# Six pairs ahead of the seven-product stage, its operands formed on VectorE, and other slots for adaLN and down

## The chip, the cores and the metric

The kernel runs on one core of a Trainium2 chip. The metric is the device time of one execution in microseconds (us), lower is better. The engines are TensorE (PE in the rows, PEld for its weight loads), VectorE (DVE), ScalarE (ACT), GpSimd (POOL) and SyncE (SP), whose queue issues nearly all DMAs here.

## The reference

Two layers of a diffusion trunk, width 1024, on 1024 latent tokens and, in layer 0, 256 context tokens. All matmuls around the change are in float32 accuracy.

```
mod = silu(c) @ w_ada[i] + b_ada[i]            # adaLN: shifts, scales, gates; 1024 x 6144
h = h + gt1 * mixer_i(modulate(rms_norm(h)))   # sliding-window attention, then neighbourhood attention
a = modulate(rms_norm(h), g_ffn, sh2, sc2)
gu = a @ w_gate_up[i]                          # 1024 x 5632
h = h + gt2 * ((silu(gu[:, :2816]) * gu[:, 2816:]) @ w_down[i])
```

## The kernel before

Activations are kept transposed: 128 channels on the partitions, 512 tokens in a row. An accurate float32 product is made of three fp32r matmuls: `split` (L140, L141) makes of a tile a high part (ScalarE's cast) and a low part (a subtraction on VectorE or GpSimd, by its argument `lo`), and low times low is left out.

**Gate and up** of the latent tokens are one product of 2 x 2 blocks (gate and up by the two halves of the channels; the two halves of the channels by the two halves of the tokens), done in seven products instead of eight. The operands on the token side are made once per layer: B11 and B21 are the normalized token half 0 (`norm_lat(0)`), T2, T3, T1, T4 and B22 are sums and differences of both halves (`norm_lat(1)`, L876 to L892, and `combine`, L894 on), each of four tiles. `f` runs over 22 pairs of a gate and an up tile. `first` makes two products (with B11 and B21), `second` one (T2), `third` four (T3, T1, T4, B22); `weights(f)` forms the weight side. A product (`product`, L793) is twelve 512-column matmuls. The first `NPRE` pairs run `first` ahead of the operand forming in program order, so that TensorE has work meanwhile; their results are held in `kp` tiles.

**Down** (L1041) takes the pairs in groups of two and then four; for each group and each half of the tokens it makes eight output tiles (steps), twelve matmuls each (six in the first group), and VectorE adds each to `h` out of its bank (`gate`, L833), of which there are four (`bm`).

**adaLN** of layer 1 (`ada`, L153) runs in layer 0's down by `tick`, one k-tile of 128 rows at a time: two DMAs of 512 KB, and four matmuls of 32 columns that fill the four column strips of the array (`j`), each recorded as two. adaLN of layer 0 runs the same way in the first stage.

SBUF tiles come from pools by tag, with a fixed number of slots: `wsp` 12 (weights), `pr` 16 (token operands), `px` 11 (`xslot`), `raw` and `rawf` 3 each (loads), `prc`/`kp` 8. T2, T3, B11 and B21 take `pr`, T1, T4 and B22 `wsp`. A compile-time planner orders the instructions of each engine: with its own model of durations it takes, at each moment, the instruction that comes first in the program among those whose inputs and slots are ready. The chip then runs each engine's and each queue's list in that order, with waits on semaphores.

Of the kernel before, what the change touches and what calls it, by code (L numbers as in the profile page):

```python
# [19 lines left out]
P = 128  # L20
# [32 lines left out]
class Trunk:  # L53
# [7 lines left out]
    def setup(self):  # L61
# [32 lines left out]
        self.hc = dr.tile([D, CTX], F32, name="hc_s")  # L94
        self.ss = [dr.tile([NF, P, SEQ], F32, name=f"s{i}_s") for i in range(2)]
# [24 lines left out]
    def unit(self, src, lo="vector", after=None, raws=None):  # L120
        nc = self.nc
        ws = []
        for i in range(2):
            s = slice(512 * i, 512 * i + 512)
            r = raws[i]() if raws else self.raw()
            if after is not None:
                nc.gpsimd.tensor_copy(out=r[0:1, 0:1], in_=after[0:1, 0:1])
            nc.sync.dma_start(out=r, in_=src[:, s])
            ws.append(self.split(r, self.slot(), lo))
        return ws  # L130
# [14 lines left out]
    def ada(self, layer, grp):  # L145
        ps = self.bank()
        for k in range(KT):
            ts = [self.slot(F32) for _ in range(2)]
            for y, t in enumerate(ts):
                self.nc.sync.dma_start(out=t.rearrange("p j n -> p (j n)"),  # L150
                                       in_=self.a["w_ada"][layer, k * P:(k + 1) * P, grp * 2048 + 1024 * y:grp * 2048 + 1024 * y + 1024])
            for j in range(4):
                self.nc.tensor.matmul(ps[32 * j:32 * j + 32, :], self.cond[:, k, :], ts[j // 2][:, j % 2], start=(k == 0), stop=(k == KT - 1))  # L153
            yield
        self.ada_close(layer, grp, ps, [(j, (32 * j, 32 * j + 2)) for j in range(4)])
        yield
# [639 lines left out]
    def back(self, layer, o):  # L796
# [68 lines left out]
        def norm_lat(c):  # L865
# [17 lines left out]
            for j in range(4):  # L883

                nc.scalar.activation(out=h[1, j], in_=h[1, j], func=AF.Identity, bias=sh[:, j, 0:1])
                nc.gpsimd.tensor_tensor(out=h[0, j], in0=h[1, j], in1=h[0, j], op=ALU.subtract)
                t2 = tmp()
                nc.vector.scalar_tensor_tensor(out=t2, in0=h[1, j + 4], scalar=sh[:, j + 4, 0:1], in1=h[0, j],
                                               op0=ALU.add, op1=ALU.subtract)
                B["t2", j] = t2  # L890
                B["T2", j] = self.split(t2, self.pslot(), alt(j))
                nc.scalar.activation(out=h[1, j + 4], in_=h[1, j + 4], func=AF.Identity, bias=sh[:, j + 4, 0:1])  # L892
                yield

        def combine():
            for j in range(4):
                nc.vector.tensor_tensor(out=h[1, j], in0=h[1, j + 4], in1=h[1, j], op=ALU.subtract)
                B["T3", j] = self.split(h[1, j], self.pslot(), alt(j))
                yield
            for j in range(4):  # L900
                B["T1", j] = self.split(h[0, j], self.slot(), alt(j))
                yield
            for j in range(4):
                nc.vector.tensor_tensor(out=h[0, j + 4], in0=h[0, j + 4], in1=B["t2", j], op=ALU.subtract)
                B["T4", j] = self.split(h[0, j + 4], self.slot(), alt(j))
                yield
            for j in range(4):
                B["B22", j] = self.split(h[1, j + 4], self.slot(), alt(j))
# [83 lines left out]
        NPRE = 3  # L992
# [11 lines left out]
        U = [first(f, ew[f]) for f in range(NPRE)]  # L1004
        w0 = weights(0)
        s0 = next(w0)
# [4 lines left out]
        for f in range(NF):  # L1011
            w = weights(f) if f else iter((s0, *w0))
            u = U[f] if f < NPRE else first(f, next(w))
# [4 lines left out]
        if not last:  # L1018
            self.later = [self.ada(1, i) for i in range(3)]
# [42 lines left out]
        for g in groups:  # L1062
            W = {f: self.unit(a["w_down"][layer, f * P:(f + 1) * P, :], "gpsimd") for f in g}
            for c in range(2):
                acts = {}
                for f in g:
                    r = rawf()
                    nc.sync.dma_start(out=r, in_=self.ss[layer][f, :, c * 512:(c + 1) * 512])
                    w = self.split(r, self.pslot(), "gpsimd")
# [3 lines left out]
                for nt in range(KT):  # L1073
# [6 lines left out]
                    if n % 3 == 0:  # L1080
# [174 lines left out]
```

## Time and profile before

| | |
|---|---|
| median of 3 runs | 2980.5 us (2977.04 to 2981.38) |
| the profiled execution | 2978.35 us, span 2976.6 us |
| TensorE busy | 2873.6 us, 97% |
| VectorE / ScalarE / GpSimd busy | 51% / 38% / 42% |
| mean granted TensorE clock | 0.986 |
| DMA | 392.66 MB, 132 GB/s in the mean |

The shares are means over stages with different limits. A busy TensorE is not yet one at its peak: after a wait its clock can be granted low, and the same matmuls take longer. A row of the order in time gives the start, the length, the engine, the line, the operation, the tile written and those read, the count, and in brackets the idle time before it and what ended that. "x" before a number counts instructions.

### The profile page before, as it was taken

The numbers are of one execution on the slowest core, as the hardware profiler recorded it, in microseconds if no ns is written. First come the engines' busy times: TensorE is split into PE (matmuls) and PEld (weight loads), VectorE is DVE, ScalarE is ACT, GpSimd is POOL, SyncE is SP. The second block draws the span as 40 slices with busy tenths as digits, with TensorE's granted clock in tenths as the row PEclk, the third lists the DMA queues.
The fourth block names the chain that finished last, engine by engine and source line by source line (L and its number), as shares of the span: only waits on it lengthen the run. The fifth ranks groups of instructions, "written<-read, shape, count | busy, mean of one in ns | idle before, by whom it ended". The sixth has DMA issues, their size and how long they took to land.

```text
span 2976.6 us, 42736 instructions
## 1 busy us (share of the span) xinstructions
PE 2873.6 (97%) x15586; PEld 2308.6 (78%) x15586; DVE 1525.0 (51%) x2643; ACT 1124.3 (38%) x2263; POOL 1237.0 (42%) x1124
## 2 busy tenths in 40 slices
PE   5999999997999999999999999999998899999999
PEld 3667767786888886778998888777787788887887
DVE  5656777558555442226543344266656755553222
ACT  4323666434332232224553223266644333323120
POOL 3443242127544545433873354011103755556440
PEclk8999999998999999999999999999999999999999
DMA  7573342531222247544553464366652222226321
GB/s 261 195 220 92 96 127 75 169 112 60 89 82 80 83 145 258 195 166 136 184 187 106 131 168 120 118 156 160 179 172 97 82 85 84 83 82 196 94 89 61
DMA packets 299843, 392.66 MB, mean 132 GB/s; under 512 B 29424, under 2 KB 165104, under 8 KB 299632
## 3 DMA queue, kind: packets, MB, share of 16 engines
q1 hardware_dynamic: 230736, 351.37, 37.2%
q10 hardware_dynamic: 68896, 38.55, 4.5%
q8 instruction: 123, 2.02, 0.3%
q14 instruction: 88, 0.72, 0.1%
HBM read 310.39 MB, written 79.43 MB: 131 GB/s over the span
## 4 chain that ended last, share of the span: by engine, by line
PE 84%; DVE 7%; DMA 4%; POOL 2%; issue 1%; ACT 1%; SPq 1%; DVEq 0%; ACTq 0%; POOLq 0%
PE bm L1041 16%; PE b L793 14%; PE bm L793 11%; PE bm L343 10%; PE bm L851 7%; PE bm L1102 4%; PE b L589 3%; PE b L343 3%; PE b L579 2%; PE b L731 2%; PE b L1041 2%; PE b L716 2%; DMA qst<-q_s 2%; PE b L153 2%; PE b L688 1%
## 5 line engine op out<-in xcount | busy, mean ns | idle before, releaser
L1041 PE MATMUL bm<-pr,wsp 128*128 128x512 f32 x2112 | 493.8, 393 | 4.5 <-DVE px L833 4.5
L1041 PEld LDWEIGHTS bm<-pr,wsp 128*128 128x128 f32 x2112 | 396.3, 189 | 111.6 <-DVE px L833 23.3
L793 PE MATMUL b<-wsp,px 128*128 128x512 f32 x1584 | 379.5, 393 | 2.8 <-DVE kp L1139 2.8
L793 PE MATMUL bm<-pr,px 128*128 128x512 f32 x1440 | 356.5, 396 | 19.3 <-DVE pr L141 11.1
L833 DVE SCALAR_TENSOR_TENSOR px<-bm,mod,px 128x512 f32<-128x512 f32 (+1 forms) x232 | 171.1, 741 | 388.6 <-PE bm L1041 336.0
L793 PEld LDWEIGHTS b<-wsp,px 128*128 128x128 f32 x1584 | 299.2, 189 | 69.5 <-DVE kp L1139 3.6
L141 POOL TENSOR_TENSOR wsp<-raw,wsp 128x512 fp32r<-128x512 f32 x186 | 241.4, 1308 | 249.2 <-ACT wsp L140 231.6
L141 POOL TENSOR_TENSOR px<-wt,px 128x512 fp32r<-128x512 f32 x176 | 237.9, 1364 | 243.1 <-ACT px L140 235.7
L793 PEld LDWEIGHTS bm<-pr,px 128*128 128x128 f32 x1440 | 272.7, 190 | 82.3 <-DVE pr L141 12.9
L140 ACT CAST wsp<-raw 128x512 fp32r<-128x512 f32 x302 | 184.9, 619 | 342.1 <-PE bm L1041 99.9
L343 PE MATMUL bm<-wsp,pr 128*128 128x512 f32 x1152 | 272.4, 393 | 0.0
L343 PEld LDWEIGHTS bm<-wsp,pr 128*128 128x128 f32 x1152 | 213.5, 188 | 43.3
L140 ACT CAST px<-wt 128x512 fp32r<-128x512 f32 x176 | 108.6, 621 | 349.0 <-PE b L793 319.0
L851 PE MATMUL bm<-pr,wsp 128*128 128x512 f32 x768 | 176.8, 390 | 0.0
L283 POOL TENSOR_TENSOR hrs<-hss,mhalf 128x8 f32<-128x8 f32 (+1 forms) x66 | 104.3, 1581 | 172.3 <-DVE hss L281 170.5
L141 POOL TENSOR_TENSOR pr<-rawf,pr 128x512 fp32r<-128x512 f32 x88 | 114.4, 1318 | 134.9 <-ACT pr L140 133.7
L343 PE MATMUL b<-wsp,pr 128*128 128x512 f32 x576 | 150.4, 414 | 18.3 <-ACT pr L252 6.1
L851 PEld LDWEIGHTS bm<-pr,wsp 128*128 128x128 f32 x768 | 143.3, 188 | 29.3
L343 PEld LDWEIGHTS b<-wsp,pr 128*128 128x128 f32 x576 | 110.3, 197 | 58.6 <-issue 13.3
L696 DVE CUSTOM_DVE_ANT_0 pr<-b,wsp,big 128x640 f32<-128x640 f32 (+1 forms) x128 | 107.5, 846 | 87.3 <-PE b L691 86.5
L141 POOL TENSOR_TENSOR px<-raw,px 128x512 fp32r<-128x512 f32 x76 | 110.2, 1452 | 91.6 <-ACT px L140 91.6
L1139 DVE TENSOR_TENSOR t<-b,kp 128x512 f32<-128x512 f32 x88 | 60.3, 685 | 169.3 <-PE b L793 169.3
(198 smaller groups left out, 4869.5 us busy)
## 6 DMA issues: line engine op xcount, KB each, us to landing
wsp<-w_ada SPq DMA_DIRECT2D x96, 512.0 KB, 6.2
qst<-q_s SPq DMA_DIRECT2D x288, 128.0 KB, 3.1
raw<-w_gu SPq DMA_DIRECT2D x144, 256.0 KB, 2.7
rawf<-w_gu SPq DMA_DIRECT2D x132, 256.0 KB, 3.0
raw<-w_down SPq DMA_DIRECT2D x110, 256.0 KB, 3.0
s_s<-t SPq DMA_DIRECT2D x88, 256.0 KB, 2.0
rawf<-s_s SPq DMA_DIRECT2D x88, 256.0 KB, 3.1
raw<-w_qkv SPq DMA_DIRECT2D x72, 256.0 KB, 3.3
```

The costliest lines, as they stand in the source:

```text
L140: self.nc.scalar.copy(out=w[:, 0, :n], in_=x)
L141: getattr(self.nc, lo).tensor_tensor(out=w[:, 1, :n], in0=x, in1=f32(w[:, 0, :n]), op=ALU.subtract)
L283: nc.gpsimd.tensor_tensor(out=rs[:, :nh], in0=ss[:, :nh], in1=self.mhalf[:, :nh], op=ALU.pow)
L343: self.nc.tensor.matmul(ps, x, y, start=(k == 0 and i == 0), stop=(k == KT - 1 and i == 2))
L589: nc.tensor.matmul(op[64 * r:64 * r + 64, :256], u["v"][:, kt, :], u["pt"][i][:, 256 * r:256 * r + 256], start=(i == 0), stop=(i == len(kt ...
L696: nc.vector.tensor_tensor_reduce(out=pt[:, :nl + 256], in0=V, in1=u["bias"][x][m // 7][:, b0:b0 + nl + 256], scale=-1.0, scalar=self.big, ...
L793: self.nc.tensor.matmul(ps, x, y, start=first and k == 0 and i == 0, stop=last and k == 3 and i == 2, skip_group_check=True)
L833: nc.vector.scalar_tensor_tensor(out=h[c, k], in0=ps, scalar=mod[:, ty, k, z:z + 1], in1=h[c, k], op0=ALU.mult, op1=ALU.add)
L851: nc.tensor.matmul(ps[:, :n], x, y, start=(k == 0 and i == 0), stop=(k == KT - 1 and i == 2))
L1041: nc.tensor.matmul(ps, x, y, start=(z == 0 and i == 0), stop=(z == len(parts) - 1 and i == 2))
L1102: nc.tensor.matmul(ps[:, q * CTX:(q + 1) * CTX], x, y, start=(k == 0 and i == 0), stop=(k == KT - 1 and i == 2))
L1139: self.nc.vector.tensor_tensor(out=out, in0=x, in1=y, op=op)
```

## The change

`norm_lat(1)` forms the difference of the two halves in one VectorE instruction from the shifted sum, instead of ScalarE and GpSimd, and all splits of T2, T3, T1, T4 and B22 put their subtraction on VectorE (`alt` put every second one on GpSimd). `NPRE` goes from 3 to 6: pairs 3 to 5 store their two tiles in device memory and load them back in the loop. Pair 0's weights are no longer begun ahead of the operand forming. `ada` can take several k-tiles at a time and another slot tag; its matmuls begin with the tile that is loaded last, and the others are held behind that one. Layer 1's adaLN takes two k-tiles at a time, from `pr`, at every fifth step of down instead of every third. In down, the weights of pairs 0 and 1 take `pr` slots instead of `wsp`, and the splits alternate between GpSimd and VectorE.

```diff
+        self.us = [dr.tile([NF, 2, P, 512], F32, name=f"u{i}_s") for i in range(2)]
...
-    def unit(self, src, lo="vector", after=None, raws=None):
+    def unit(self, src, lo="vector", after=None, raws=None, slot=None):
...
-            ws.append(self.split(r, self.slot(), lo))
+            ws.append(self.split(r, (slot or self.slot)(), lo))
...
-    def ada(self, layer, grp):
+    def ada(self, layer, grp, slot=None, n=1):
         ps = self.bank()
-        for k in range(KT):
-            ts = [self.slot(F32) for _ in range(2)]
-            for y, t in enumerate(ts):
-                self.nc.sync.dma_start(out=t.rearrange("p j n -> p (j n)"),
-                                       in_=self.a["w_ada"][layer, k * P:(k + 1) * P, grp * 2048 + 1024 * y:grp * 2048 + 1024 * y + 1024])
-            for j in range(4):
-                self.nc.tensor.matmul(ps[32 * j:32 * j + 32, :], self.cond[:, k, :], ts[j // 2][:, j % 2], start=(k == 0), stop=(k == KT - 1))
+        for k0 in range(0, KT, n):
+            ts = {}
+            for k in range(k0, k0 + n):
+                for y in range(2):
+                    ts[k, y] = (slot or self.slot)(F32)
+                    self.nc.sync.dma_start(out=ts[k, y].rearrange("p j n -> p (j n)"),
+                                           in_=self.a["w_ada"][layer, k * P:(k + 1) * P, grp * 2048 + 1024 * y:grp * 2048 + 1024 * y + 1024])
+            with ExitStack() as order:
+                for k in range(k0 + n - 1, k0 - 1, -1):
+                    for j in (2, 3, 0, 1):
+                        m = self.nc.tensor.matmul(ps[32 * j:32 * j + 32, :], self.cond[:, k, :], ts[k, j // 2][:, j % 2],
+                                                  start=(k == n - 1), stop=(k == KT - n))
+                        if k == k0 + n - 1 and j == 2:
+                            order.enter_context(self.tc.issue_after(getattr(m, "ins", m)))
...
-                nc.scalar.activation(out=h[1, j], in_=h[1, j], func=AF.Identity, bias=sh[:, j, 0:1])
-                nc.gpsimd.tensor_tensor(out=h[0, j], in0=h[1, j], in1=h[0, j], op=ALU.subtract)
+                nc.vector.scalar_tensor_tensor(out=h[0, j], in0=h[1, j], scalar=sh[:, j, 0:1], in1=h[0, j],
+                                               op0=ALU.add, op1=ALU.subtract)
...
-                B["T2", j] = self.split(t2, self.pslot(), alt(j))
-                nc.scalar.activation(out=h[1, j + 4], in_=h[1, j + 4], func=AF.Identity, bias=sh[:, j + 4, 0:1])
+                B["T2", j] = self.split(t2, self.pslot(), "vector")
+                for k in (j, j + 4):
+                    nc.scalar.activation(out=h[1, k], in_=h[1, k], func=AF.Identity, bias=sh[:, k, 0:1])
...
-                B["T3", j] = self.split(h[1, j], self.pslot(), alt(j))
+                B["T3", j] = self.split(h[1, j], self.pslot(), "vector")
...
-        NPRE = 3
+        NPRE, HELD = 6, 3
...
-        U = [first(f, ew[f]) for f in range(NPRE)]
-        w0 = weights(0)
-        s0 = next(w0)
+        U = []
+        for f in range(NPRE):
+            U.append(first(f, ew[f]))
+            if f >= HELD:
+                for i in range(2):
+                    nc.sync.dma_start(out=self.us[layer][f, i], in_=U[f][i])
...
-            w = weights(f) if f else iter((s0, *w0))
-            u = U[f] if f < NPRE else first(f, next(w))
+            w = weights(f)
+            if f >= NPRE:
+                u = first(f, next(w))
+            elif f < HELD:
+                u = U[f]
+            else:
+                u = keep(), keep()
+                for i in range(2):
+                    nc.sync.dma_start(out=u[i], in_=self.us[layer][f, i])
...
-            self.later = [self.ada(1, i) for i in range(3)]
+            self.later = [self.ada(1, i, self.pslot, 2) for i in range(3)]
...
-            W = {f: self.unit(a["w_down"][layer, f * P:(f + 1) * P, :], "gpsimd") for f in g}
+            W = {f: self.unit(a["w_down"][layer, f * P:(f + 1) * P, :], alt(f), slot=self.slot if f > 1 else self.pslot) for f in g}
...
-                    w = self.split(r, self.pslot(), "gpsimd")
+                    w = self.split(r, self.pslot(), alt(f + 1))
...
-                    if n % 3 == 0:
+                    if n % 5 == 0:
```

The splits of T1, T4 and B22 change as that of T3 does.

## Rows read from the trace of the kernel before

**Rows 1.** The page's first part: busy us, share of the span, instructions.

```profile
PE 2873.6 (97%) x15586; PEld 2308.6 (78%) x15586; DVE 1525.0 (51%) x2643; ACT 1124.3 (38%) x2263; POOL 1237.0 (42%) x1124
```

**Rows 2.** Busy time in equal stretches of 50 us: the stretch, its length, then busy us and instructions of PE, PEld, DVE, ACT and POOL, the granted TensorE clock, the DMA engines' busy share and GB/s. The start of down in layer 0, the head of the seven-product stage in layer 1, and an undisturbed stretch of the seven-product stage.

```profile
1100.00:1150.00 50.00, 45.95 (x196) 31.54 (x195) 17.22 (x23) 15.91 (x28) 28.15 (x22) 0.97 0.90 313
2300.00:2350.00 50.00, 37.04 (x134) 28.13 (x135) 47.92 (x43) 21.47 (x39) 43.35 (x27) 0.83 0.17 58
2400.00:2450.00 50.00, 50.00 (x220) 41.01 (x220) 26.48 (x30) 16.01 (x28) 26.43 (x20) 1.00 0.26 90
```

**Rows 3.** The same columns, for the head of the seven-product stage in layer 0 and in layer 1, and for the operand chain on VectorE in layer 1.

```profile
670.98:746.62 75.64, 60.14 (x239) 46.07 (x238) 63.76 (x64) 33.26 (x59) 56.51 (x36) 0.89 0.19 63
2278.85:2354.95 76.10, 60.68 (x242) 46.90 (x240) 63.36 (x62) 32.67 (x57) 55.65 (x35) 0.89 0.19 66
2291.27:2326.46 35.19, 21.30 (x64) 14.60 (x62) 35.19 (x30) 21.23 (x37) 29.37 (x19) 0.76 0.02 8
```

**Rows 4.** TensorE in order of time, the head in layer 1 (L784: the transposes that release the chain).

```profile
2278.85 6.96 PE L793 MATMUL bm<-pr,wsp 128*128 128x512 f32 x30
...
2286.46 4.33 PE L793 MATMUL bm<-pr,wsp 128*128 128x512 f32 x18
2290.63 0.60 PE L784 MATMUL b<-ident,rs 128*128 128x128 f32 x4
...
2295.16 3.04 PE L793 MATMUL bm<-pr,wsp 128*128 128x512 f32 x12 [1.16 <-ACT kp L951]
...
2302.10 1.65 PE L793 MATMUL bm<-pr,px 128*128 128x512 f32 x3 [3.33 <-POOL pr L141]
2308.97 2.93 PE L793 MATMUL bm<-pr,px 128*128 128x512 f32 x6 [5.22 <-DVE pr L141]
2311.69 0.63 PE L793 MATMUL b<-pr,px 128*128 128x512 f32 x1
```

**Rows 5.** TensorE in order of time, the head in layer 0 (L774 at 659.42: the sums of the latent norm).

```profile
659.42 0.95 PE L774 MATMUL b<-ones,acc 128*128 128x2 f32 x8
...
670.98 6.08 PE L793 MATMUL bm<-pr,wsp 128*128 128x512 f32 x26
...
677.26 5.24 PE L793 MATMUL bm<-pr,wsp 128*128 128x512 f32 x22
682.34 0.60 PE L784 MATMUL b<-ident,rs 128*128 128x128 f32 x4
```

**Rows 6.** VectorE in order of time, the operand chain in layer 1.

```profile
2291.27 5.36 DVE L876 SCALAR_TENSOR_TENSOR px<-px,gsc,b 128x512 f32<-128x512 f32 x8 [3.87 <-PE b L784]
...
2308.84 0.68 DVE L897 TENSOR_TENSOR px<-px 128x512 f32<-128x512 f32 x1
2309.44 1.77 DVE L904 TENSOR_TENSOR px<-px,t 128x512 f32<-128x512 f32 x1
```

**Rows 7.** GpSimd in order of time, the same stretch.

```profile
2295.71 1.30 POOL L141 TENSOR_TENSOR wsp<-px,wsp 128x512 fp32r<-128x512 f32 x1 [0.26 <-ACT wsp L140]
...
2300.34 1.71 POOL L141 TENSOR_TENSOR pr<-t,pr 128x512 fp32r<-128x512 f32 x1
```

**Rows 8.** TensorE in order of time, the start of down in layer 1.

```profile
2727.58 3.79 PE L1041 MATMUL bm<-pr,wsp 128*128 128x512 f32 x16
2735.82 29.39 PE L1041 MATMUL bm<-pr,wsp 128*128 128x512 f32 x116 [4.45 <-DVE px L833]
```

**Rows 9.** VectorE in order of time, the same place.

```profile
2733.60 1.50 DVE L1139 TENSOR_TENSOR t<-t,kp 128x512 f32<-128x512 f32 x1 [5.13 <-ACT t L988]
2735.03 2.71 DVE L833 SCALAR_TENSOR_TENSOR px<-bm,mod,px 128x512 f32<-128x512 f32 x4
```

**Rows 10.** ScalarE in order of time, the same place.

```profile
2732.42 0.62 ACT L140 CAST wsp<-raw 128x512 fp32r<-128x512 f32 x1 [1.28 <-DMA raw<-w_down]
2732.95 0.62 ACT L988 ACTIVATE t<-t 128x512 f32<-128x512 f32 x1
```

**Rows 11.** TensorE in order of time, down in layer 0: the start, two stretches of four column matmuls, then one of eight.

```profile
1127.09 1.78 PE L153 MATMUL b<-wsp,cond 128*32 128x512 f32 x4 [4.05 <-DMA wsp<-w_ada]
...
1137.74 1.05 PE L153 MATMUL b<-wsp,cond 128*32 128x512 f32 x4
1138.73 1.67 PE L1041 MATMUL bm<-pr,wsp 128*128 128x512 f32 x6
...
1256.68 8.46 PE L1041 MATMUL bm<-pr,wsp 128*128 128x512 f32 x36
1265.07 1.06 PE L153 MATMUL b<-wsp,cond 128*32 128x512 f32 x8
1266.06 8.46 PE L1041 MATMUL bm<-pr,wsp 128*128 128x512 f32 x36
```

**Rows 12.** TensorE in order of time, the first stage: two k-tiles of adaLN one behind the other.

```profile
168.42 1.92 PE L153 MATMUL b<-wsp,cond 128*32 128x512 f32 x16
170.28 3.48 PE L343 MATMUL b<-wsp,pr 128*128 128x512 f32 x14
```

**Rows 13.** L153 alone in two stretches, the first stage and layer 0's down: length, busy us and instructions of PE and PEld, granted clock, DMA share, GB/s.

```profile
100.00:222.00 122.00, 24.30 (x128) 3.75 (x128) 1.00 0.77 239
1119.00:1352.00 233.00, 31.49 (x192) 4.43 (x192) 0.99 0.59 200
```

**Rows 14.** Whom ScalarE waited for from 1100 to 1360 us (layer 0's down): us in total, times, the longest.

```profile
ACT pr L140 <- DMA rawf<-s_s: 46.7, 13, 9.5
```

More of the change, by code (lines that the diff above doesn't have):

```diff
@@ L897, in combine @@
                 nc.vector.tensor_tensor(out=h[1, j], in0=h[1, j + 4], in1=h[1, j], op=ALU.subtract)
-                B["T3", j] = self.split(h[1, j], self.pslot(), alt(j))
+                B["T3", j] = self.split(h[1, j], self.pslot(), "vector")
                 yield
             for j in range(4):
-                B["T1", j] = self.split(h[0, j], self.slot(), alt(j))
+                B["T1", j] = self.split(h[0, j], self.slot(), "vector")
                 yield
@@ L904, in combine @@
                 nc.vector.tensor_tensor(out=h[0, j + 4], in0=h[0, j + 4], in1=B["t2", j], op=ALU.subtract)
-                B["T4", j] = self.split(h[0, j + 4], self.slot(), alt(j))
+                B["T4", j] = self.split(h[0, j + 4], self.slot(), "vector")
                 yield
             for j in range(4):
-                B["B22", j] = self.split(h[1, j + 4], self.slot(), alt(j))
+                B["B22", j] = self.split(h[1, j + 4], self.slot(), "vector")
                 yield
```

## The prediction

> **What bounds the kernel now.** I read the page first: TensorE is busy for 97% of the span [rows 1], so a change can only win where TensorE waits, where its clock is granted low, or where it does work twice. The table of busy time in equal stretches then shows where that is. An undisturbed 50 us hold 220 matmuls at a granted clock of 1.00 [rows 2], which is 50 / 220 = 0.2273 us for each 512-column matmul, 2.73 us for a product of twelve. Two kinds of stretch fall short: the head of the seven-product stage in each layer (0.83 in one of them) and the start of the down stage, where the DMA engines are at 0.90 [rows 2].
>
> In the head, from the first matmul of pair 0's first product on, I asked for one stretch in each layer [rows 3]. Each holds three pairs' first two products and thirteen more products, 19 x 12 = 228 large matmuls, or 51.8 us, and about 1 us of small ones. They take 75.64 and 76.10 us, at a mean granted clock of 0.89. So **23 us are lost per layer**. [...]
>
> What TensorE waits for is a chain on VectorE that is busy without a pause from 2291.27 to 2326.46: 30 instructions in 35.19 us, beside 29.37 us of GpSimd [rows 3]. The two get in each other's way: a VectorE subtraction takes 0.68 us (0.60 from start to start) with GpSimd idle and 1.77 beside it [rows 6], a GpSimd one 1.30 or 1.71 [rows 7].
>
> **The chain without GpSimd.** The change gives VectorE all twenty subtractions of `split` (ten before) and folds the four GpSimd subtractions of L886 into four fused VectorE instructions. VectorE then has 16 fused ones (8 of L876, 4 new, 4 of L888) at 5.36 / 8 = 0.67 us and 28 plain ones at 0.60 [rows 6]: 10.7 + 16.8 = 27.5 us, against 35.2. GpSimd keeps only weight splits there, and most of those wait for an `xslot` that T4's operands free. From the chain's start the operands are ready at 13.1 us (T2: 16 x 0.67 + 4 x 0.60), 17.9 (T3), 20.3 (T1), 25.1 (T4) and 27.5 (B22).
>
> [...] Rows price the same subtraction at 1.30 on one engine and 0.60 on the other, so I count on the shorter chain.
>
> **More cover.** Pairs 3 to 5 move their first two products (six products, 16.4 us) ahead of the chain's results; TensorE's work stays the same in all. How much of the twelve products still lies behind the chain's start decides. The chain starts when four transposes (L784) have run, and these come after the products in program order. In both layers they ran after exactly 48 matmuls [rows 4, 5], in layer 0 although the sums that they need were taken 11 us before the first product. So the planner puts them where it finds no product ready. With three pairs that was where a second product waited for ScalarE to empty its bank (1.16 us in the trace [rows 4]). With six pairs pair 3's first product fills that hole; the next holes are after five products or, once four banks are in use, after seven. So the chain starts 13.6 + 1.2 = 14.8 us after the first product, or 20.3, against 12.4 now.
>
> Behind the start lie then seven products (19.1 us) or five (13.6), with some three waits of 1.16 us, 3.5 in all, at the end, where nothing is left to fill them. T2 (13.1) is hidden in both. In the late case TensorE ends the pairs at 17.1, T2's product at 19.8, T3's and T1's at 25.3; T4's adds into a bank that VectorE must first read, two additions that queue behind the chain, at 28.7: a wait of 3.4, and some 3 us at low clock after it. Loss 3.5 in the early case, 9.9 in the late one, against 23. I take 7: **16 us saved per layer, 32 in all**, bounds 26 and 39. Its other costs are hidden: six stores and six loads of 256 KB per layer and six weight halves loaded twice lie where the DMA engines are at 0.26 [rows 2]; the stores wait on SP for ScalarE's evacuation, with weight loads queued behind them, which are needed only after twelve products. The extra VectorE subtractions for pairs 3 to 5 fall before the chain. If GpSimd worked through the chain after all, the price is that of the second rival.
>
> **Down's start.** In layer 1 TensorE stops for 4.45 us with all four banks full, and the next 116 matmuls take 29.39 us instead of 26.4 [rows 8]: 7.5 us. The bank is late because VectorE's product of the stage before waited 5.13 us for ScalarE's Silu [rows 9], which stood behind a cast waiting for a `w_down` load [rows 10]. That load was late because its weights take `wsp` slots, which T1, T4 and B22 hold to the stage's end. Pairs 0 and 1 of `w_down` now take `pr` slots, which B11 and B21 leave with the last pair's second product. I take 6 us saved, bounds 0 (another cast blocks the Silu) and 7.5. In layer 0 the same hole is 4.05 us, ended by a `w_ada` load [rows 11], with some 2 us at low clock after it: 6. But adaLN tiles are now asked for 2.1 MB at a time, one batch in five steps of 1.36 us, 308 GB/s where the DMA engines move 313 at 0.90 [rows 2]; a wait for them can come back. I take 3, bounds -6 and 6. The splits that move from GpSimd to VectorE cost nothing while four banks cover VectorE; the last rival prices that.
>
> **adaLN.** A stretch of eight column matmuls takes 0.99 us from start to start, and a stretch of four, half a k-tile, takes 0.99 too [rows 11]. Torn tiles cost twice. In down the 31.49 us of L153 [rows 13] are 29 such stretches for 24 tiles. Each also costs the neighbours 0.21 us (36 matmuls take 8.39 us between two stretches, 8.18 undisturbed [rows 11]). Two tiles together took 1.85 us [rows 12]. So 29 x 1.20 = 34.8 becomes 12 x 2.06 = 24.7: 10 us. I take 8, since part of it lies in the hole counted above, bounds 4 and 10. In the first stage 24.30 us for 16 tiles [rows 13] could become 16 x 0.99 = 15.8, 8 us less; but TensorE also waits for VectorE and loads there, so I take 4, bounds 0 and 8.
>
> **The sum.** 32 + 6 + 3 + 8 + 4 = 53 us off the profiled execution's 2978.35 gives 2925.4. The median of the runs is 2.15 above that execution: **2927 us**. All bounds at their best give 70.5 off, 2910; all at their worst 24 off, 2956.
>
> **Rivals.** (1) The transposes come after all twelve products. Nothing is then behind the chain's start: TensorE waits 13.1 for T2, 2.1 for T3, 2.6 for T4, with 3.5 between pairs and some 8 at low clock, 29 instead of 23. The head loses 12 instead of winning 32: 2971. For it: they are last in program order; against it: in both layers they found a hole. 0.12. (2) The chain stays at 35 us, because weight splits on GpSimd keep running beside it: 7.5 more per layer, 2942. For it: GpSimd's 29.37 us now; against it: 14 of its 19 instructions there are the ones that move. 0.13. (3) The head wins, but adaLN and down do not, because layer 0's down start is set by the DMA engines (0.90) and the first stage by its loads: 2948. For it: both holes there end with a load; against it: torn stretches are TensorE's own time. 0.13. (4) Slower: in down VectorE now holds splits that wait for loads, and the emptying of the banks queues behind them. ScalarE waited 46.7 us for such loads in 13 waits there, up to 9.5 [rows 14]; three free banks cover 3 x 2.73 = 8.2 us. If each of the 24 half groups of both layers lost 2.2 us, the 53 would be gone; at 3 us the time is 2999. The mean wait of 3.6 speaks against it. 0.05.
>
> **Chances and range.** The forecast has 0.57. The range of 2908 to 2958 leaves out the first and last rivals and little else. This kernel's runs tell a difference of about 0.2%, 6 us, from none. Faster by more: the forecast, rivals 2 and 3 and most of rival 1, 0.91; within it 0.04; slower 0.05.
>
> **What the profile after would show.** Right: L784 after 60 to 84 matmuls of products; VectorE's subtractions in the head at 0.68 us, the chain done in some 28 us; waits of TensorE in the head under 5 us at a clock near 1.00; L153 in stretches of sixteen in down, some 12 of them, and stretches of eight before; no hole of 4 us at either down start. Wrong: L784 after 144 matmuls, subtractions at 1.7 us, TensorE waiting for `w_ada` or for L833 within the down stages, or a first stage as long as before.

## The result, and the profile after

The changed kernel takes **2937.5 us** (median of four runs, 2932.9 to 2940.7) against 2979.1 for the kernel before on the same chip: a ratio of 0.9859, 95% interval 0.9842 to 0.9876, so 41.6 us faster. Forecast were 2927 us and a range of 2908 to 2958. The sign stands, the time lies inside the range, and the gain is 42 us where 53 were worked out; one term of the sum, the largest, was too big by 12 us, one more by 3.6, and others that came out better made up for 8 of that. The profiled execution took 2932.86 us (span 2931.0), 45.5 less than the one before.

Between landmarks on TensorE (end of the first stage, first matmul of the head, the 371st large matmul after it, where the stretches below end, first work behind the latent tokens' down, end), the two profiled executions differ like this:

| Part | forecast, us | measured, us |
|---|---|---|
| First stage (adaLN tiles together) | -4 | -5.9 |
| Attention, its projection, and the rest | 0 | -1.4 |
| Head of the seven-product stage, layer 0 | -16 | -10.1 |
| Rest of layer 0's seven products and down, with adaLN | -11 (8 + 3) | -15.8 |
| Head of the seven-product stage, layer 1 | -16 | -10.0 |
| Rest of layer 1's seven products and down | -6 | -2.4 |
| Sum | -53 | -45.6 |

The page's first part, to be held against [rows 1]:

```profile
PE 2845.3 (97%) x15586; PEld 2305.4 (79%) x15586; DVE 1596.1 (54%) x2765; ACT 1124.5 (38%) x2263; POOL 1080.0 (37%) x1002
```

TensorE has the same 15,586 matmuls and is busy for 28 us less: 14.8 of these are in the rows of adaLN's column matmuls (below), and the heads' stretches, at a mean granted clock of 0.95 where it was 0.89, lose 5 us less to matmuls that run long. GpSimd has 122 instructions fewer, and VectorE has 122 more.

**The heads.** The heads in layer 0 and layer 1 and the operand chain on VectorE in layer 1; columns as in [rows 3]:

```profile
662.80:761.18 98.38, 90.14 (x382) 73.11 (x381) 74.89 (x99) 41.61 (x75) 46.58 (x31) 0.95 0.35 118
2245.61:2344.65 99.04, 91.01 (x385) 73.92 (x384) 77.19 (x98) 41.00 (x74) 45.75 (x30) 0.95 0.34 116
2260.74:2286.97 26.23, 23.62 (x96) 18.82 (x95) 26.23 (x43) 20.52 (x38) 3.19 (x1) 0.93 0.08 30
```

Each of the two head stretches holds 371 large matmuls and 1.1 or 1.55 us of small ones. 371 x 0.2273 = 84.3, so 13.0 and 13.2 us are lost in them, against 23 before. The third row is the chain as far as it runs without a pause: 42 of its 44 instructions in 26.2 us; 35.2 before [rows 3]. TensorE in order of time, the head in layer 1 (L802 is a product, L793 the transposes that release the chain):

```profile
2254.12 6.15 PE L802 MATMUL bm<-pr,wsp 128*128 128x512 f32 x26
2260.11 0.60 PE L793 MATMUL b<-ident,rs 128*128 128x128 f32 x4
2260.46 11.17 PE L802 MATMUL bm<-pr,wsp 128*128 128x512 f32 x48
2274.24 0.71 PE L802 MATMUL bm<-pr,px 128*128 128x512 f32 x1 [2.61 <-ACT kp L964]
2274.75 4.40 PE L802 MATMUL bm<-pr,wsp 128*128 128x512 f32 x12
...
2306.28 13.87 PE L802 MATMUL b<-wsp,px 128*128 128x512 f32 x48 [5.42 <-DVE kp L1159]
```

There are two waits, 2.61 and 5.42 us, and behind each some of the matmuls run at a low granted clock, 0.50 from 2274.75 to 2277.30 and from 2306.28 to 2309.48, against 1.00 from 2312.28 on: twelve take 4.40 us where 2.73 is usual, 48 take 13.87 where 10.9 is. 2.6 + 5.4 + 1.7 + 3.0 = 12.7 of the 13.2. Layer 0 has the same two, 2.62 and 5.62, each with 0.50 behind it.

What the second wait is for stands on VectorE (order of time, layer 1; L142 is the subtraction in `split`, L1159 the helper for additions):

```profile
2260.74 5.36 DVE L885 SCALAR_TENSOR_TENSOR px<-px,gsc,b 128x512 f32<-128x512 f32 x8 [5.68 <-PE b L793]
...
2275.53 0.69 DVE L142 TENSOR_TENSOR pr<-t,pr 128x512 fp32r<-128x512 f32 x1
...
2279.74 0.69 DVE L142 TENSOR_TENSOR pr<-t,pr 128x512 fp32r<-128x512 f32 x1
...
2285.76 1.29 DVE L142 TENSOR_TENSOR pr<-px,pr 128x512 fp32r<-128x512 f32 x2
2286.97 0.69 DVE L1159 TENSOR_TENSOR kp<-bm,kp 128x512 f32<-128x512 f32 x1
2291.32 1.21 DVE L1159 TENSOR_TENSOR wt<-rawf 128x512 f32<-128x512 f32 x1 [3.67 <-POOL px L142]
...
2295.86 1.78 DVE L142 TENSOR_TENSOR wsp<-px,wsp 128x512 fp32r<-128x512 f32 x1
...
2304.88 0.74 DVE L1159 TENSOR_TENSOR wt<-rawf 128x512 f32<-128x512 f32 x1 [4.94 <-DMA rawf<-w_gu]
2305.55 0.68 DVE L1159 TENSOR_TENSOR kp<-b,kp 128x512 f32<-128x512 f32 x1
```

The chain is done at 2286.97, but for the last two of its twenty subtractions (`wsp<-px,wsp`, at 2295.86 and 2307.94), for which TensorE doesn't wait. Of the two additions ahead of T4's product, the first (`kp<-bm,kp`) runs there at once; the second, which reads the bank that T4's product adds into (`kp<-b,kp`), runs at 2305.55, 18.6 us later. In between VectorE holds weight additions of later pairs: one waits 3.67 us for a GpSimd subtraction, one 4.94 for a load of `w_gu`. The load is late by the same queue; SP in order of time:

```profile
2294.26 5.45 SPq L951 DMA_DIRECT2D raw<-w_gu  x2
2299.76 0.90 SPq L951 DMA_DIRECT2D rawf<-w_gu  x2
```

Whom it waited for from 2285 to 2306 (us in total, times, the longest):

```profile
SPq L951 <- DVE wt L1159: 9.3, 2, 4.7
```

The load that VectorE waits for is issued at 2299.76, behind a load on SP that waits for VectorE's own weight additions to leave a `raw` buffer. So the engine's late additions make its next load late, and the bank-emptying addition behind it pays.

**adaLN.** L159 alone (the column matmuls; length, busy us and instructions of PE and PEld, clock, DMA share, GB/s), beside [rows 13]:

```profile
100.00:222.00 122.00, 17.88 (x128) 2.75 (x128) 1.00 0.77 240
1100.00:1390.00 290.00, 23.08 (x192) 5.01 (x192) 0.99 0.57 193
```

TensorE in order of time at layer 0's down start, beside [rows 11]:

```profile
1101.58 4.47 PE L1061 MATMUL bm<-pr 128*128 128x512 f32 x19
1105.97 1.92 PE L159 MATMUL b<-pr,cond 128*32 128x512 f32 x16
1107.83 7.13 PE L1061 MATMUL bm<-pr 128*128 128x512 f32 x30
```

The 24 tiles of down take 23.08 us in twelve stretches of sixteen, 31.49 in 29 stretches before; TensorE waits for nothing from there to the end of the latent tokens' down. In layer 1's down start the hole has turned into smaller ones:

```profile
2691.48 1.65 PE L1061 MATMUL bm<-pr 128*128 128x512 f32 x6 [1.95 <-DVE px L842]
2693.34 1.65 PE L1061 MATMUL bm<-pr 128*128 128x512 f32 x6 [0.21 <-DVE px L842]
2695.21 7.39 PE L1061 MATMUL bm<-pr 128*128 128x512 f32 x30 [0.21 <-DVE px L842]
2703.78 5.73 PE L1061 MATMUL bm<-pr 128*128 128x512 f32 x24 [1.17 <-DVE px L842]
```

That is 3.5 us in four waits, 4.45 in one before [rows 8]. Two of VectorE's instructions ahead of the last wait say why:

```profile
2699.53 0.69 DVE L142 TENSOR_TENSOR wsp<-raw,wsp 128x512 fp32r<-128x512 f32 x1 [2.41 <-ACT wsp L141]
2700.14 0.75 DVE L842 SCALAR_TENSOR_TENSOR px<-bm,mod,px 128x512 f32<-128x512 f32 x1
```

The gating instruction L842, which empties a bank, stands behind a weight split that the change moved to VectorE and that waits for ScalarE's cast.

### The profile page after: what moved, and what is told of

Its sections match the earlier page's. It is cut to its first block, busy times and chain, and to the rows that moved or that the text cites. A ratio compares the mean times of both kernels' runs of the same rounds, so it can differ in the third digit from the quotient of the medians.

```text
span 2931.0 us, 42778 instructions
## 1 busy us (share of the span) xinstructions
PE 2845.3 (97%) x15586; PEld 2305.4 (79%) x15586; DVE 1596.1 (54%) x2765; ACT 1124.5 (38%) x2263; POOL 1080.0 (37%) x1002
## 4 chain that ended last, share of the span: by engine, by line
PE 86%; DVE 4%; DMA 4%; ACT 2%; POOL 2%; issue 1%; SPq 1%; DVEq 0%; POOLq 0%; ACTq 0%
PE b L802 16%; PE bm L1061 16%; PE bm L802 10%; PE bm L352 10%; PE bm L860 7%; PE bm L1122 4%; PE b L352 3%; PE b L598 3%; PE b L588 3%; PE b L740 2%; PE b L1061 2%; PE b L725 2%; DMA qst<-q_s 2%; PE b L555 1%; PE b L159 1%
## 5 line engine op out<-in xcount | busy, mean ns | idle before, releaser
L1061 PE MATMUL bm<-pr,wsp 128*128 128x512 f32 x1920 | 440.3, 390 | 0.0
L1061 PEld LDWEIGHTS bm<-pr,wsp 128*128 128x128 f32 x1920 | 359.2, 188 | 82.1 <-issue 6.7
L802 PE MATMUL b<-wsp,px 128*128 128x512 f32 x1584 | 382.0, 395 | 11.0 <-DVE kp L1159 11.0
L802 PEld LDWEIGHTS b<-wsp,px 128*128 128x128 f32 x1584 | 300.9, 190 | 78.1 <-DVE kp L1159 11.9
L142 POOL TENSOR_TENSOR px<-wt,px 128x512 fp32r<-128x512 f32 x176 | 237.1, 1360 | 246.9 <-ACT px L141 238.9
L842 DVE SCALAR_TENSOR_TENSOR px<-bm,mod,px 128x512 f32<-128x512 f32 (+1 forms) x232 | 170.7, 739 | 279.8 <-PE bm L1061 223.5
L802 PE MATMUL bm<-pr,px 128*128 128x512 f32 x1296 | 317.3, 392 | 5.2 <-ACT kp L964 5.2
L142 POOL TENSOR_TENSOR wsp<-raw,wsp 128x512 fp32r<-128x512 f32 x144 | 191.7, 1339 | 299.6 <-ACT wsp L141 270.9
L802 PEld LDWEIGHTS bm<-pr,px 128*128 128x128 f32 x1296 | 243.4, 188 | 59.4 <-ACT kp L964 6.1
L142 DVE TENSOR_TENSOR wsp<-raw,wsp 128x512 fp32r<-128x512 f32 x162 | 133.4, 829 | 138.7 <-ACT wsp L141 138.7
L860 PE MATMUL bm<-pr,wsp 128*128 128x512 f32 x768 | 176.8, 390 | 1.0 <-DVE ot L604 1.0
L860 PEld LDWEIGHTS bm<-pr,wsp 128*128 128x128 f32 x768 | 143.3, 188 | 30.6 <-DVE ot L604 1.2
L1159 DVE TENSOR_TENSOR t<-b,kp 128x512 f32<-128x512 f32 x88 | 60.3, 685 | 144.3 <-PE b L802 144.3
L1122 PE MATMUL bm<-prc,wsp 128*128 128x256 f32 x1056 | 133.6, 285 | 0.0
```

The lines of the kernel that those rows point to most:

```text
L142: getattr(self.nc, lo).tensor_tensor(out=w[:, 1, :n], in0=x, in1=f32(w[:, 0, :n]), op=ALU.subtract)
L802: self.nc.tensor.matmul(ps, x, y, start=first and k == 0 and i == 0, stop=last and k == 3 and i == 2, skip_group_check=True)
L842: nc.vector.scalar_tensor_tensor(out=h[c, k], in0=ps, scalar=mod[:, ty, k, z:z + 1], in1=h[c, k], op0=ALU.mult, op1=ALU.add)
L860: nc.tensor.matmul(ps[:, :n], x, y, start=(k == 0 and i == 0), stop=(k == KT - 1 and i == 2))
L1061: nc.tensor.matmul(ps, x, y, start=(z == 0 and i == 0), stop=(z == len(parts) - 1 and i == 2))
L1122: nc.tensor.matmul(ps[:, q * CTX:(q + 1) * CTX], x, y, start=(k == 0 and i == 0), stop=(k == KT - 1 and i == 2))
```

## The experiments

Each ratio is to the kernel before, measured beside it on the same chip. Stage differences are those of the profiled execution against that of the kernel before, the heads and the first stage between the landmarks of the table above; layer 0's down and "layer 1's last part" are counted from the last matmul of the seven products.

**One part alone: adaLN.** The kernel before with the new `ada` and its two calls:

```
-            self.later = [self.ada(1, i) for i in range(3)]
+            self.later = [self.ada(1, i, self.pslot, 2) for i in range(3)]
...
-                    if n % 3 == 0:
+                    if n % 5 == 0:
                         self.tick()
```

> The kernel before with the adaLN part alone (two k-tiles together from the pr slots at every fifth step of down, a k-tile's four column matmuls kept together in the first stage). My theory, that torn tiles are TensorE's own time: L153 stretches fall to 12 in down and 16 in the first stage, the first stage is 6 us shorter and layer 0's down 10 us, about 2963 us in all; the heads and layer 1's down keep their time. Rival, that these stretches lie in the shadow of loads: L153's busy time falls, but TensorE waits for w_ada instead and the time stays within 4 us of before.

Measured: 2964.8 us, ratio 0.9945 (0.9928 to 0.9961). The first stage is 4.9 us shorter, layer 0's down 12.9. So adaLN is worth what was forecast for it and for the hole together, and layer 0's down start closes with it alone: no load holds it. The expected twelve stretches didn't come: two batches of the twelve are still torn, and the tiles take 25.58 us in 16 stretches.

**One part alone: operands on VectorE**, with three pairs ahead as before:

```
-                nc.gpsimd.tensor_tensor(out=h[0, j], in0=h[1, j], in1=h[0, j], op=ALU.subtract)
+                nc.vector.scalar_tensor_tensor(out=h[0, j], in0=h[1, j], scalar=sh[:, j, 0:1], in1=h[0, j],
+                                               op0=ALU.add, op1=ALU.subtract)
...
-                B["T3", j] = self.split(h[1, j], self.pslot(), alt(j))
+                B["T3", j] = self.split(h[1, j], self.pslot(), "vector")
```

> The kernel before with the operands formed on VectorE alone, three pairs ahead as before. If cover and a short chain are both needed: the chain falls from 35 us to 27, but TensorE reaches T2's product 6 us too early and T4's 5 us too early, so each head wins about 3 us (loss 20 of 23), 2973 us. Rival, that the short chain is all that counts: each head wins the 9.4 us of the full change, 2960 us.

Measured: 2975.6, 0.9978 (0.9966 to 0.9989); the two heads are 3.2 and 3.8 us shorter. TensorE's waits in layer 1's head, the longest ones:

```profile
PE bm L793 <- ACT pr L140: 4.8, 1, 4.8
PE bm L793 <- DVE pr L141: 3.6, 1, 3.6
PE bm L793 <- POOL px L141: 3.3, 1, 3.3
```

The shorter chain alone leaves TensorE waiting for T2 (the first two waits), since three pairs cover too little of it, and then for a weight split on GpSimd.

**One part alone: six pairs ahead**, with the subtractions alternating between the engines as before:

```
-        NPRE = 3
+        NPRE, HELD = 6, 3
```

> The kernel before with six pairs ahead and their spill alone, the operand subtractions alternating between VectorE and GpSimd as before. If both are needed: the chain stays near 35 us with subtractions of 1.7 us, TensorE runs out of products 22 us after the chain's start and then waits for T2 and T3, each head wins about 5 us, 2969 us. Rival, that cover is all that counts: each head wins the 9.4 us of the full change, 2960 us.

Measured: 2968.3, 0.9953 (0.9936 to 0.9971); heads 6.3 and 7.8 us shorter. The longest waits of layer 1's head:

```profile
PE bm L794 <- ACT kp L955: 4.8, 1, 4.8
PE b L794 <- DVE kp L1150: 4.5, 2, 3.1
```

The time is as expected, the mechanism is not: TensorE waits for banks and not for T2 or T3. More cover alone is worth twice the shorter chain alone. Together the two won 10.1 and 10.0 (9.5 and 9.3 counted to the end of the seven products); the two alone add up to 9.5 and 11.6, so neither stands in for the other. And the wait for a bank-emptying addition (`kp`) already stands here, with the subtractions half on GpSimd: it comes with the six pairs.

**Down's splits back on GpSimd**, everything else as changed (the first two `w_down` tiles still in `pr` slots):

```
-            W = {f: self.unit(a["w_down"][layer, f * P:(f + 1) * P, :], alt(f), slot=self.slot if f > 1 else self.pslot) for f in g}
+            W = {f: self.unit(a["w_down"][layer, f * P:(f + 1) * P, :], "gpsimd", slot=self.slot if f > 1 else self.pslot) for f in g}
...
-                    w = self.split(r, self.pslot(), alt(f + 1))
+                    w = self.split(r, self.pslot(), "gpsimd")
```

> The changed kernel with all splits of down on GpSimd again; the weights of pairs 0 and 1 stay in pr slots. If the 3.5 us that TensorE still waits at the start of layer 1's down come from VectorE's emptying of the banks standing behind splits that wait for loads: these waits are gone and the time falls by 3 to 5 us. Rival, that the loads themselves are late: ScalarE's Silu or TensorE's own operands are waited for instead, and the time stays or rises.

Measured: 2936.8, 0.9852 (0.9826 to 0.9877). Layer 1's last part is 6.6 us shorter than before the change, where the change itself had 3.1 by the same landmark, and TensorE's 3.5 us of waits there have become one:

```profile
PE bm L1061 <- DVE px L842: 1.3, 1, 1.3
```

So the moved splits cost 3.5 us in layer 1's down. The totals differ by less than their intervals; the place in the trace carries this verdict.

**The down part undone**: those splits on GpSimd, and the first two `w_down` tiles in `wsp` slots again:

```
-            W = {f: self.unit(a["w_down"][layer, f * P:(f + 1) * P, :], alt(f), slot=self.slot if f > 1 else self.pslot) for f in g}
+            W = {f: self.unit(a["w_down"][layer, f * P:(f + 1) * P, :], "gpsimd") for f in g}
...
-                    w = self.split(r, self.pslot(), alt(f + 1))
+                    w = self.split(r, self.pslot(), "gpsimd")
```

> The changed kernel with the down part of the change undone: all splits in down on GpSimd, and the first two w_down tiles in wsp slots again. Theory: with adaLN's tiles together and nothing else, layer 0's down won 12.9 us of the 16.4 of the whole change; the down part is the rest, 3.5, and the 3.0 that layer 1's down won: 2937.5 + 6.5 = 2944, with a wait of TensorE of about 4 us, all banks full, at layer 1's down start. Rival: the heads' new order of work frees the wsp slots sooner by itself, the late w_down load is gone with the old slots too, and the time is within 2 us of 2937.

Measured: 2941.3, 0.9861 (0.9842 to 0.9879). The hole is back where it was, on TensorE in layer 1:

```profile
2701.83 18.34 PE L1061 MATMUL bm<-pr,wsp 128*128 128x512 f32 x70 [5.01 <-DVE px L842]
```

Layer 0's down is 12.9 us shorter than before the change, as with adaLN alone, and not 16.5: its column tiles are torn again (25.31 us in 16 stretches). With the splits alone taken back they are not (23.08), so the 3.6 us there are won by the `pr` slots. Layer 1's last part is as long as before the change, against 3.1 shorter as changed and 6.6 with the splits alone taken back. So in layer 1's down the `pr` slots win some 6 us (0.7 of the 6.6 are three matmuls of down that now run ahead of the landmark), and the splits on VectorE give 3.5 of them back. The two downs together are 6.7 us longer than as changed, as the theory had it; layer 1's head is 2.0 shorter here, with a wait of 3.1 for the bank in the place of 5.4, because VectorE's order there came out a little different, and the interval of the total can't tell 2941 from 2944.

**adaLN one tile at a time**, tiles still kept together:

```
-            self.later = [self.ada(1, i, self.pslot, 2) for i in range(3)]
+            self.later = [self.ada(1, i, self.pslot) for i in range(3)]
...
-                    if n % 5 == 0:
+                    if n % 3 == 0:
```

> The changed kernel with layer 1's adaLN, which runs within layer 0's down, taken one k-tile at a time (every third step) and not two (every fifth): its column tiles are still kept together, in stretches of eight. By the prediction's price, 24 stretches x (0.99 + 0.21) = 28.8 us in the place of 12 x (1.85 + 0.21) = 24.7: 4 us more, 2941.5, all of it in layer 0's down. If what counted was only that tiles are no longer torn, the time stays within 2 us of 2937.5. If smaller batches suit the loads better (1 MB at a time and not 2.1), layer 0's down could be shorter by a few us: 2935.

Measured: 2944.7, 0.9867 (0.9847 to 0.9887). L159 in layer 0's down (columns as above):

```profile
1100.00:1390.00 290.00, 26.61 (x192) 3.91 (x192) 1.00 0.57 196
```

3.5 us more in its own rows, and 13 more interruptions of 0.21 us each make 2.7: 6.2. Layer 0's down is 5.3 longer than as changed. Pairing the tiles is worth 5, keeping them together the rest. What the total shows beyond that lies where the two kernels are alike (6.0 us of the profiled execution in the first stage, 1.9 in attention), so the verdict is the stage's, not the total's.

**The order on VectorE.** The weight additions of pairs 2 to 7 are queued behind an addition that empties a bank of the pair two before (`U3[f]` is the one that reads pair f's T1 product):

```
+        def nxt(w, f):
+            with ExitStack() as order:
+                if 2 <= f < 8:
+                    order.enter_context(tc.issue_after(U3[f - 2]))
+                return next(w)
...
-            second(u[0], next(w))
-            third(f, *u, next(w))
+            second(u[0], nxt(w, f))
+            third(f, *u, nxt(w, f))
```

> The changed kernel with another order on VectorE in the head of the seven-product stage: the additions of weight pairs 2 to 7 are queued behind the additions that empty the banks of the pair two before, so that no weight addition that waits for a load stands ahead of them. TensorE's order stays. Theory A (the waits of 5.62 and 5.42 us in the two heads come from bank-emptying additions that stand behind weight additions, which wait for loads of w_gu): both waits fall under 1.5 us, and with them some of the matmuls at half clock; each head loses about 8 us where it lost 13, and the time is 2927 (2937.5 - 2 x 5). Theory B (TensorE has simply run out of cover, and the chain ends too late for T4's products): the waits stay, with another releaser, and the time stays at 2937. A third possibility: the weight additions come too late in their new place and TensorE waits for the weights of pairs 2 and 3 instead, 2937 or more.

Measured: **2920.4**, 0.9791 (0.9773 to 0.9810), 17 us faster than as changed. The two heads:

```profile
669.59:768.16 98.57, 95.48 (x419) 77.30 (x418) 76.56 (x100) 43.77 (x79) 50.68 (x33) 1.00 0.38 122
2240.72:2340.10 99.38, 96.78 (x422) 79.12 (x421) 78.36 (x100) 43.25 (x78) 50.04 (x32) 0.98 0.36 119
```

A stretch as long as before now holds 408 large matmuls and not 371. Lost are 98.57 - 92.74 - 1.10 = 4.7 us and 99.38 - 92.74 - 1.55 = 5.1, where 13 were lost. The waits of 5.62 and 5.42 are gone, TensorE waits 0.3 us for weights in layer 0 and not at all in layer 1, where one wait is left:

```profile
PE bm L802 <- ACT kp L964: 2.6, 1, 2.6
```

Theory A holds, by more than it said: the wait, the low clock after it (the mean over the head was 0.95 and is 1.00 and 0.98), and no new wait.

**The transposes earlier.** `next(g1)` once more ahead of the first products:

```
+        next(g1)
         U = []
         for f in range(NPRE):
```

> The changed kernel with the four transposes that release the operand chain moved ahead of pair 0's products in program order. In layer 0 they then run after some 34 matmuls of products and not after 60, 5.9 us earlier; in layer 1 the sums that they need come late, and nothing moves. Theory A (bank-emptying additions behind weight additions that wait for loads): the loads come when they came, so layer 0's wait of 5.62 us stays within 1.5 us, and the time is 2937. Theory B (the chain ends too late): layer 0's wait is gone with a chain that ends 5.9 us sooner, and the time is 2931.

Measured: 2936.0, 0.9841 (0.9824 to 0.9859). In layer 0 the transposes run after 34 matmuls, but the chain starts only 3.5 us sooner and not 5.9, since VectorE is still at weight additions, and the head loses 12.8 us (13.0 as changed). TensorE's waits there:

```profile
PE bm L802 <- ACT kp L964: 4.6, 1, 4.6
PE bm L802 <- DVE kp L1160: 2.2, 1, 2.2
```

The wait for T4's bank is gone, as theory B asked, and the time is not: ScalarE's emptying of a bank falls into the chain's casts and is 2.0 us later, and VectorE's falls into the weight additions at another place. Neither theory has it quite. In layer 1 the head is 2.2 us shorter than as changed, with the second wait at 4.1 us. An earlier chain doesn't help layer 0 while the bank-emptying instructions have no place in the order.

**Both orders together.** The VectorE order as above (`nxt`), and down's splits on GpSimd:

```
+            second(u[0], nxt(w, f))
...
+                    w = self.split(r, self.pslot(), "gpsimd")
```

> The kernel with the additions reordered in the head, and all of down's splits on GpSimd as before the change (the first two w_down tiles stay in pr slots). The reordered heads alone gave 2920.4; in layer 1's down TensorE then still waited 3.3 us for gating instructions that stand behind splits on VectorE. Theory (both are separate holes): the 3.3 falls under 1.5 and the time is 2917 to 2919. Rival (the gates are late for another reason, now that the heads are shorter): 2920 to 2922.

Measured: **2916.6** (five runs, 2915.0 to 2924.2), 0.9792 (0.9777 to 0.9806): the fastest version here, 21 us below the changed kernel and 66 below the kernel before beside it. Layer 1's last part is 6.3 us shorter than before (2.4 with the VectorE order alone), and TensorE's wait there 1.5 us, 3.3 without the second edit.

**And ScalarE's order too.** The version above, with the eight activations of L902 queued behind the Silu that empties pair 2's bank (`SG` holds the Silu of each pair):

```
-                for k in (j, j + 4):
-                    nc.scalar.activation(out=h[1, k], in_=h[1, k], func=AF.Identity, bias=sh[:, k, 0:1])
+                with tc.issue_after(SG[2]):
+                    for k in (j, j + 4):
+                        nc.scalar.activation(out=h[1, k], in_=h[1, k], func=AF.Identity, bias=sh[:, k, 0:1])
```

> The kernel of the run before with one more order, on ScalarE: the eight activations of L902 (the shift of the second half's operands, needed for T3 and B22 alone) are queued behind the Silu that empties pair 2's bank. Theory: the one wait left in each head, 2.6 us for ScalarE's bank-emptying, comes from that run of activations and casts standing ahead of it, and the twelve matmuls at half clock come from the wait (4.6 us in the place of 2.75); both go, 2.6 + 1.8 = 4.4 us less per layer, 8 to 9 in all: 2909 to 2911. Rival: T3's and B22's operands come that much later, TensorE waits for those instead, and the time stays at 2917 to 2920.

Measured: 2919.3, 0.9794 (0.9780 to 0.9807): no gain. In layer 1's head TensorE waits

```profile
PE bm L802 <- DVE pr L142: 1.9, 1, 1.9
PE bm L802 <- ACT kp L965: 0.7, 1, 0.7
```

The wait of 2.6 shrinks to 0.7, and 1.9 come back as a wait for one of T2's subtractions; against the version above, layer 1's head is 0.8 us shorter and layer 0's 1.2 longer. That is the rival's case, though with T2 and not T3 or B22. What is left in the heads, some 5 us each, no run here took away.

## Why the prediction was right, and where it was not

**What bounds the kernel**: right. TensorE has the same matmuls and is busy 28 us less; the other 17 us of the 45.6 are idle time. Of the 28, the column matmuls give 14.8 (24.30 and 31.49 us became 17.88 and 23.08), and what is left is for the most part fewer matmuls at a low granted clock (0.50 behind the waits) and fewer interruptions.

**The chain without GpSimd**: right. 27.5 us were forecast for 44 instructions; 42 of them took 26.2, and two more at 0.60 would make it 27.4, with subtractions at 0.68 or 0.69 us and GpSimd at 3.19 us of work beside it, where it had 29.37. The move helped because the work left an engine that took 1.30 us for it, and beside which VectorE took 1.77. One detail of the working failed: T2 was to be ready 13.1 us after the start and was at 19.7, since the order of VectorE isn't that of the program (T1's and some of T4's instructions ran before T2's subtractions). Six pairs covered that: TensorE doesn't wait for T2.

**Where the transposes run**: right, the early case: after exactly 60 matmuls in both layers, 14.1 and 14.5 us after the first product began; the chain starts at 14.7 and 15.1 (14.8 forecast).

**More cover: the term that was mis-sized.** Each head was to lose 7 us, within 3.5 and 9.9, and lost 13. The step that failed is the one on T4: it "adds into a bank VectorE must first read, two additions that queue behind the chain", with a wait of 3.4 in the late case only. The place was right, the queue was not: the first addition ran right behind the chain, but the second stood behind the weight additions of pairs 2 and 3 too, which wait for GpSimd and for loads, and came 18.6 us after the first (7.2 in the reordered kernel). With it fell the sentence that the loads behind the stores on SP are needed "only after twelve products": TensorE needs them then, but VectorE asks for them sooner and holds its queue for them. The run that reorders these additions loses 4.7 and 5.1 us per head, inside the forecast's bounds: so the cover was counted rightly, and 8 us per layer is what VectorE's order cost.

The three waits of 1.16 us between pairs became one of 2.6, with 1.3 and 1.7 us lost at low clock behind it (0.50 granted at first). The run with ScalarE reordered shows that it can be moved and not won. The forecast's terms at low clock were estimates. The late case's 3 us stand behind the wait for T4, and behind the waits of 5.62 and 5.42 us there 2.7 and 3.0 were lost, with 0.50 granted at first; the first rival's 8 no run shows.

**Down's start in layer 1**: the `pr` slots win some 6 us, as I took; the hole is back without them. It was not the `w_down` load alone: of the casts that stand ahead of the Silu [rows 10], one waits for a slot that TensorE leaves late:

```profile
2730.52 0.62 ACT L140 CAST wsp<-raw 128x512 fp32r<-128x512 f32 x1 [1.06 <-PE bm L1041]
```

What failed is a term put at nothing: the sentence that the moved splits "cost nothing while four banks cover VectorE" was wrong there. They cost 3.5, so the part won 2.4 and not 6. This is the fourth rival's mechanism, in one of the two layers and at a twentieth of the 72 us between its time and the forecast.

**Layer 0's down and adaLN**: better than forecast, 15.8 for 11. The rows of L159 fell by 8.4, and 17 fewer interruptions at 0.21 make 3.6: 12.0, where I had worked out 10 and counted 8; some 3 of the 12 come only with the `pr` slots of down, as the runs with adaLN alone and with the down part undone show. The remaining 3.8 are the hole of 4.05, of which I counted 3 for fear of a wait for 2.1 MB at once. There is none. The third rival is out.

**First stage**: 4 forecast, 5.9 measured in this execution; in the nine profiled kernels with the new first stage it lay between 0.2 us longer and 5.9 shorter than before, 3.7 shorter in the mean (two with the old one stood at +0.2 and +3.0). So some 2 of the 5.9, and the 1.4 of attention, where nothing was changed, are luck, and they hide as much of what the heads fell short.

**The stores**: SP does stand in front of them with weight loads behind, 18.8 and 6.1 us in layer 1. Whom SP waited for from 2255 to 2306 us:

```profile
SPq L1019 <- ACT kp L961: 18.8, 1, 18.8
SPq L951 <- POOL px L142: 8.5, 2, 6.3
```

But the load behind the first three stores then waits 6.3 us more, until a GpSimd subtraction has left its buffer, so the stores did not make it late. The reordered kernel has the same waits for the stores (17.8 and 6.7), and TensorE waits for weights there 0.3 us at most.

**The signs named**: those of right came (the transposes after 60 matmuls, subtractions at 0.68, twelve stretches of sixteen, no hole of 4 us), but for one: TensorE's waits in a head are 8 us at a clock of 0.95, not under 5 near 1.00. And one sign of wrong came in part: TensorE waits in layer 1's down for the gating instruction (L833, now L842), 3.5 us.

## What to carry to other kernels

When work is moved ahead to cover a chain, list what stands in the chain's engine directly behind it: the short instruction that empties a bank must not queue behind one that waits for a load (here TensorE waited 5.42 and 5.62 us for it). A load that is early enough for TensorE can be too late for the engine that prepares it, as VectorE's wait of 4.94 us was here; ask for both. And when an edit bundles several parts, price each by its own stage: here two parts that won were bundled with one move (splits onto VectorE in down) that lost 3.5 us, hidden in a total that was 42 better.

## What the runs showed of the hardware

GpSimd in order of time in the changed kernel, its first subtraction beside the end of the chain:

```profile
2283.78 4.43 POOL L142 TENSOR_TENSOR px<-rawf,px 128x512 fp32r<-128x512 f32 x1 [27.86 <-ACT px L141]
2288.17 5.51 POOL L142 TENSOR_TENSOR px<-wt,px 128x512 fp32r<-128x512 f32 x4
```

It takes 4.43 us, 4.39 to the start of the next; the four behind it 1.38 each, and one took 1.30 before [rows 7]. VectorE, at 0.60 from start to start, is not slowed at all. Until 2286.97 it runs subtractions that read two SBUF tiles, six of them beside this one; then comes an addition that reads a bank and one SBUF tile, and the GpSimd instruction ends 1.24 us after that addition began. Layer 0 shows 4.51 at the same place, the reordered kernel 4.45 in layer 1, and there the end comes 1.26 and 1.23 us after the addition began. So in these three places the GpSimd instruction ends about the time of one, 1.3 us, after VectorE's run of such subtractions does, and only one of the two engines is slowed, over six instructions of the other. In other places both are slowed (1.77 for VectorE, 1.71 for GpSimd [rows 6, 7]). No run here was made to tell what decides between them, so that stays open. It is not free: the 6.3 us that SP waits with the next load, above, are for this instruction.
